# A gated MLP's down product, regrouped from plain block products into seven products of half blocks

## The chip, the cores and the metric

The kernel runs on one core of one Trainium2 chip. The metric is the device time of one execution in microseconds (us). Engines are named as in the profile: PE is TensorE (matmuls), PEld its weight load, DVE is VectorE, ACT is ScalarE, POOL is GpSimd, and SP is SyncE, which here only issues transfers.

## The reference, cut to what matters

The program is a decoder trunk of two layers over 1024 positions with a model width of 1024. Each layer mixes the sequence in four head groups, then runs a gated MLP with a short causal convolution, then adds a gated embedding. The part that is changed is the last matrix product of the MLP:

```python
D_MODEL, SEQ, DEPTH, D_FF = 1024, 1024, 2, 2816

def conv_ffn(x, w_up, conv_w, conv_b, w_down):
    up = x @ w_up                                  # 1024 -> 2 * 2816
    ...                                            # causal convolution over 3 positions
    gate, val = jnp.split(conv, 2, axis=-1)
    return (jax.nn.silu(gate) * val) @ w_down      # 2816 -> 1024

h = h + conv_ffn(rmsnorm(h, ffn_norm_g[i]), ...)
ple_gate = jax.nn.sigmoid(rmsnorm(h, ple_norm_g[i]) @ w_ple_gate[i])
h = h + ple_gate * (p[i] @ w_ple[i])
```

All inputs and the output are float32.

## The kernel before, in words

Everything is kept transposed: features lie on the 128 partitions, the 1024 positions along the free dimension, in two halves of 512. The 1024 model features are 8 blocks (index `m`), the 2816 hidden features are 22 blocks (`NFF`, index `f`).

Each float32 operand of a matmul is split in two parts that TensorE takes at its fast float32 rate: `hi`, a rounded copy, and `lo`, what the copy left over (`lo = x - hi`, helper `K.lo`, line 103, on whichever engine it is given). A product of two such operands is three matmuls: hi by hi, hi by lo, lo by hi (lines 1476 to 1478). One such matmul has a 128x128 block of weights and 512 positions.

`ffn_up` (lines 1304 to 1437) computes the up product. It already takes it as seven products of half blocks (`SEQ`, line 1301) instead of eight: sums of quarter blocks of weights and of activations are formed on VectorE, each of the seven is computed, and the results are recombined. It stores the 22 blocks of `hidden` in device memory (`hid`, line 1375).

`Down.load` (lines 1447 to 1463) prepares one of 44 operand sets: it issues the transfer of one 128x1024 block of `w_down` (tile `wr`, 512 KB) and of one 128x512 half block of `hid` (tile `g`, 256 KB), copies both hi parts on ScalarE, forms the `lo` of `g` on VectorE, and the `lo` of the weights in two halves on GpSimd. `Down.run` (lines 1465 to 1486) takes the left half of the positions and then the right one. For each it runs over the 22 blocks `f`, with 8 x 3 matmuls each into 8 PSUM banks; then VectorE adds the 8 banks to the residual tiles `h` (line 1484), and `done` hands each to the next normalization (`Norm.add`, lines 801 to 814: a scaled hi copy and a square on ScalarE, a `lo` part on VectorE, and sums of squares on VectorE and GpSimd in turn). After `Down.run` the gate product `pg` of the embedding follows (lines 762 to 764).

What sets the order of the work is the supply of tiles. Tiles come from pools with fixed numbers of buffers: 2 for `wr`, 6 for `wx` (the hi and lo of weights, two to a set, so 3 sets), 8 for the wide tiles that hold the pair hi and lo of `g` (also used by the convolution), 71 for half tiles (tag `h`), 8 PSUM banks. `T['dl']=4` is the number of sets that the code writes down ahead of the matmuls. The order on each engine is fixed when the program is built, from the order of the code and from what is then thought to be ready first; on the chip each engine runs its list in order and waits on semaphores.

Of the kernel before, what the change touches and what calls it, by code (L numbers as in the profile page):

```python
# [8 lines left out]
F32 = mybir.dt.float32  # L9
F32R = mybir.dt.float32r  # L10
# [4 lines left out]
ALU = mybir.AluOpType  # L15
# [4 lines left out]
P = 128  # L20
S = 1024
HS = 512
D = 1024
KD = D // P
DEPTH = 2
NFF = 22
# [15 lines left out]
T = dict(early=(0, 0.2), s5=((0.1, 0.7), (0.1, 0.7)), hgrn=((0.2, 0.92), (0.2, 0.92)), cd=((0.05, 0.85), (0.05, 0.85)), prep=((0.3, 1), (0.3, 1)), b=(0, 1), a=(0.9, 0.95), pre=(8, 10, 12, 13), vals=(5, 6), ahead=3, plv=4, mx=8, pw=1, rt=2, sc=2, rp=6, dl=4, qk=(4, 4), up=5)  # L42


class Kern:
    def __init__(self, tc, ctx, halves=71):
        self.tc, self.nc = tc, tc.nc
        self.n, self.turn = 0, False
        self.other = []
        self.cp = ctx.enter_context(tc.tile_pool(name="cp", bufs=1))  # L50
        self.sp = ctx.enter_context(tc.tile_pool(name="sp", bufs=2))
        self.pp = ctx.enter_context(tc.tile_pool(name="pp", bufs=2, space=PSUM))
        self.halves = halves
# [51 lines left out]
    def after(self, i, u):  # L105
        self.tc.add_manual_dep(i.ins, u.ins.name, mybir.DependencyInfo(
            mybir.DependencyClass.NoSync, mybir.DependencyReason.DATA), reason="order")
# [627 lines left out]
def rows(wh, wl, k, m=P):  # L735

    return wh[:, k * m:(k + 1) * m], wl[:, k * m:(k + 1) * m]

def wraw(K, src, n=S, blocks=1):
    raw = K.sp.tile([P, n], F32, name=K._nm("wr"), tag="wr", bufs=2)  # L740
    K.nc.sync.dma_start(raw if blocks == 1 else raw.rearrange("p (k m) -> p k m", k=blocks), src)
    return raw
# [36 lines left out]
class Norm:  # L779
# [11 lines left out]
    def add(self, i, n, x):  # L791
        self.parts(i, n, x)
        self.square(i, n, x)
# [77 lines left out]
def run(gen):  # L871
    for _ in gen:
        pass
# [149 lines left out]
def attention(heads):  # L1023
# [10 lines left out]
    for _ in b.prep():  # L1034
        yield
    run(a.values())
    for i in range(len(heads)):
        nxt, pre = get(i + 2), iter(())
        mx, vals = (b.max(), b.values()) if b else (iter(()), iter(()))
        for step, _ in enumerate(a.out()):  # L1040
            for _ in range(2 if step % 2 or step < T['mx'] else 1):
                next(mx, None)
            if step == 6 and nxt:
                while nxt() is None:
                    yield
                nxt = nxt()
                pre = nxt.prep()
            if step in T['pre']:
                next(pre, None)
            if step in T['vals']:  # L1050
                next(vals, None)
            yield
        for g in (mx, vals, pre):
            run(g)
        a, b = b, nxt
# [168 lines left out]
class Quarters:  # L1224
# [22 lines left out]
    def flush(self, n=0):  # L1247

        for t in self.todo[:len(self.todo) - n]:
            if len(t) == 4:  # L1250
                self.K.nc.scalar.copy(t[3], t[2])
            self.K.lo(*t[:4])
        self.todo = self.todo[len(self.todo) - n:]
        for t in self.todo:
            if len(t) == 4:
                self.K.nc.scalar.copy(t[3], t[2])
                t.append(True)
# [182 lines left out]
class Down:  # L1440

    def __init__(self, K, hid, w_down):
        self.K, self.hid, self.w, self.ops = K, hid, w_down, []

    def load(self):

        K, nc = self.K, self.K.nc
        V, G = nc.vector, nc.gpsimd  # L1450
        n, f = divmod(len(self.ops), NFF)
        if n == 2:
            return
        r, g = wraw(K, self.w[f]), K.h(name="g")
        nc.sync.dma_start(g, self.hid[f][:, n * HS:(n + 1) * HS])
        hi, lo = K.wx(), K.wx()
        gh, gl = K.pair(F32R, "g")
        nc.scalar.copy(gh, g)  # L1458
        nc.scalar.copy(hi, r)  # L1459
        K.lo(V, gl, g, gh)  # L1460
        for c in (slice(0, HS), slice(HS, S)):
            K.lo(G, lo[:, c], r[:, c], hi[:, c])
        self.ops.append(((hi, lo), (gh, gl)))

    def run(self, h, hdr, done):
        K, nc = self.K, self.K.nc
        V = nc.vector
        for n in range(2):
            ps = [b("dn") for b in (K.pf, K.pf, K.po, K.po, K.px, K.px, K.px, K.px)]
            for f in range(NFF):  # L1470
                while len(self.ops) < min(n * NFF + f + T['dl'], 2 * NFF):
                    self.load()
                w, (gh, gl) = self.ops[n * NFF + f]
                for m in range(KD):
                    ah, al = rows(*w, m)
                    nc.tensor.matmul(ps[m], lhsT=ah, rhs=gh, start=f == 0, stop=False)  # L1476
                    nc.tensor.matmul(ps[m], lhsT=ah, rhs=gl, start=False, stop=False)  # L1477
                    nc.tensor.matmul(ps[m], lhsT=al, rhs=gh, start=False, stop=f == NFF - 1)  # L1478
                m = f - NFF + KD + 4
                if 0 <= m < KD:  # L1480
                    h[m][n] = K.h(name="h")
                    nc.sync.dma_start(h[m][n], hdr[m][:, n * HS:(n + 1) * HS])
            for m in range(KD):
                V.tensor_tensor(h[m][n], h[m][n], ps[m], op=ALU.add)
            for m in range(KD):
                done(m, n)


@with_exitstack
def body(ctx, tc, xT, pT, pos, invf, sgn, vecs, prms, dsk, bfs, w_fm, w_misc, w_tm, w_uq, w_ukv, w_glu,  # L1490
# [29 lines left out]
    def first(l):  # L1520

        uf, z = [K.two(name="uf") for _ in range(2)], K.two(name="z")
        scaled = lambda t: lambda n, ps: V.tensor_tensor(t[n], ps, nm.r(n), op=ALU.mult)
        run(proj(K, [w_fm[l, i] for i in FIRST], nm.xs, [scaled(t) for t in uf + [z]], banks=[K.pf, K.pf, K.po],
                 ws=None if l else ws))
        return uf, z
# [413 lines left out]
```

## Time and profile before

| | |
|---|---|
| median of 3 runs | 3009.31 us (3005.92 to 3016.06) |
| the profiled execution's own time | 3008.91 us |
| its span in the trace | 3007.2 us |
| PE, PEld busy | 2819.5 us (94%), 2270.8 us (76%) |
| DVE, ACT, POOL busy | 2139.2 us (71%), 1417.9 us (47%), 1060.5 us (35%) |
| matmuls of `Down` (lines 1476 to 1478) | 3 x 704 |
| share of the chain that ended last | PE 61%, DVE 21% |

Busy time is the sum of an engine's instructions. Matmuls are pipelined, so one that is 390 ns long can start 227 ns after the one before it; the distance of starts is what counts for time. The chain is the work that ended last, followed back from the last instruction to what released it.

### The profile page before, as it was taken

The numbers are of one execution on the slowest core, as the hardware profiler recorded it, in microseconds if no ns is written. First come the engines' busy times: TensorE is split into PE (matmuls) and PEld (weight loads), VectorE is DVE, ScalarE is ACT, GpSimd is POOL, SyncE is SP. The second block draws the span as 40 slices with busy tenths as digits, with TensorE's granted clock in tenths as the row PEclk, the third lists the DMA queues.
The fourth block names the chain that finished last, engine by engine and source line by source line (L and its number), as shares of the span: only waits on it lengthen the run. The fifth ranks groups of instructions, "written<-read, shape, count | busy, mean of one in ns | idle before, by whom it ended". The sixth has DMA issues, their size and how long they took to land.

```text
span 3007.2 us, 37310 instructions
## 1 busy us (share of the span) xinstructions
PE 2819.5 (94%) x13346; PEld 2270.8 (76%) x13346; DVE 2139.2 (71%) x3130; ACT 1417.9 (47%) x2435; POOL 1060.5 (35%) x919
## 2 busy tenths in 40 slices
PE   8889899898999999999999898988989999999997
PEld 6777676676788888888787786766667888888886
DVE  7795767658999997253847776666599999953358
ACT  4235356665544444242733263666554444443345
POOL 2620123445322224555423201324452222255554
PEclk9898899999999999999998798999999999999998
DMA  3101011104222226353421011110132222262523
GB/s 127 38 23 43 29 59 56 38 8 148 70 84 85 84 85 207 98 192 98 156 67 32 21 50 49 57 55 22 46 126 74 85 84 85 77 221 94 190 102 130
DMA packets 115850, 255.14 MB, mean 85 GB/s; under 512 B 18544, under 2 KB 21232, under 8 KB 115664
## 3 DMA queue, kind: packets, MB, share of 16 engines
q1 hardware_dynamic: 114224, 252.10, 25.2%
q8 instruction: 105, 1.72, 0.2%
q10 hardware_dynamic: 1440, 0.65, 0.1%
q14 instruction: 81, 0.66, 0.1%
HBM read 197.58 MB, written 48.50 MB: 82 GB/s over the span
## 4 chain that ended last, share of the span: by engine, by line
PE 61%; DVE 21%; issue 8%; ACT 6%; POOL 3%; DMA 1%; SPq 0%; DVEq 0%; POOLq 0%; ACTq 0%
PE up L1358 8%; PE up L1356 8%; PE up L1357 8%; PE dn L1477 5%; PE dn L1476 5%; PE dn L1478 5%; PE qk L1006 2%; PE pj L774 2%; PE pj L775 2%; PE pj L776 2%; DVE wx L103 1%; DVE xq L1237 1%; PE ys L633 1%; DVE qz L286 1%; DVE bl L103 1%
## 5 line engine op out<-in xcount | busy, mean ns | idle before, releaser
L103 POOL TENSOR_TENSOR wx<-wr,wx 128x512 fp32r<-128x512 f32 (+1 forms) x293 | 485.9, 1671 | 351.0 <-ACT wx L1459 200.0
L1356 PE MATMUL up<-bh,wx 128*128 128x512 f32 x1232 | 481.3, 391 | 12.2 <-ACT wx L1349 12.2
L1357 PE MATMUL up<-bl,wx 128*128 128x512 f32 x1232 | 481.9, 391 | 8.6 <-POOL bl L103 4.5
L1358 PE MATMUL up<-bh,wx 128*128 128x512 f32 x1232 | 482.0, 391 | 6.3 <-DVE wx L103 6.3
L1356 PEld LDWEIGHTS up<-bh,wx 128*128 128x128 f32 x1232 | 232.6, 189 | 61.2 <-ACT wx L1349 13.1
L1477 PE MATMUL dn<-g,wx 128*128 128x512 f32 x704 | 274.7, 390 | 3.8 <-DVE g L103 3.8
L1357 PEld LDWEIGHTS up<-bl,wx 128*128 128x128 f32 x1232 | 232.7, 189 | 58.9 <-POOL bl L103 5.4
L103 POOL TENSOR_TENSOR pl<-pr,ph 128x512 fp32r<-128x512 f32 x144 | 164.3, 1150 | 314.9 <-ACT pr L1012 251.5
L1358 PEld LDWEIGHTS up<-bh,wx 128*128 128x128 f32 x1232 | 232.4, 189 | 56.5 <-DVE wx L103 8.3
L1476 PE MATMUL dn<-g,wx 128*128 128x512 f32 x704 | 274.6, 390 | 0.0
L1478 PE MATMUL dn<-g,wx 128*128 128x512 f32 x704 | 274.5, 390 | 0.0
L103 DVE TENSOR_TENSOR g<-g,g 128x512 fp32r<-128x512 f32 x88 | 105.1, 1210 | 204.5 <-ACT g L1458 196.2
L103 POOL TENSOR_TENSOR wx<-wq,wx 128x512 fp32r<-128x512 f32 x44 | 65.2, 1483 | 515.9 <-ACT wx L1349 515.9
L774 PE MATMUL pj<-xs,wx 128*128 128x512 f32 (+1 forms) x512 | 211.7, 414 | 15.3 <-ACT xs L801 7.0
L1459 ACT CAST wx<-wr 128x1024 fp32r<-128x1024 f32 x88 | 92.4, 1050 | 277.2 <-PE dn L1477 260.5
L775 PE MATMUL pj<-xs,wx 128*128 128x512 f32 (+1 forms) x512 | 207.2, 405 | 0.9 <-DVE xs L802 0.9
L776 PE MATMUL pj<-xs,wx 128*128 128x512 f32 (+1 forms) x512 | 207.0, 405 | 0.8 <-DVE wx L103 0.5
L1477 PEld LDWEIGHTS dn<-g,wx 128*128 128x128 f32 x704 | 132.6, 188 | 32.1 <-DVE g L103 4.7
L1476 PEld LDWEIGHTS dn<-g,wx 128*128 128x128 f32 x704 | 132.5, 188 | 27.8
L1478 PEld LDWEIGHTS dn<-g,wx 128*128 128x128 f32 x704 | 132.5, 188 | 27.5
L1367 DVE SCALAR_TENSOR_TENSOR cv<-u,vec,cv 128x1023 f32<-128x1023 f32 x88 | 131.0, 1491 | 28.1 <-ACT cv L1366 27.8
L103 POOL TENSOR_TENSOR yl<-xn,yh 128x512 fp32r<-128x512 f32 x24 | 35.8, 1493 | 293.8 <-ACT yh L862 293.8
(464 smaller groups left out, 6972.0 us busy)
## 6 DMA issues: line engine op xcount, KB each, us to landing
wr<-in_w_down SPq DMA_DIRECT2D x88, 512.0 KB
wr<-in_w_up SPq DMA_DIRECT2D x88, 256.0 KB
wq<-in_w_up SPq DMA_DIRECT2D x88, 256.0 KB
hid<-cv SPq DMA_DIRECT2D x44, 512.0 KB
g<-hid SPq DMA_DIRECT2D x88, 256.0 KB
wr<-in_w_fm SPq DMA_DIRECT2D x30, 512.0 KB
wr<-in_w_pg SPq DMA_DIRECT2D x28, 512.0 KB
hdr<-h SPq DMA_DIRECT2D x48, 256.0 KB
```

Of the source, the lines that this page charges most:

```text
L103: eng.tensor_tensor(out, x, hi.bitcast(F32), op=ALU.subtract)
L774: nc.tensor.matmul(out, lhsT=ah, rhs=bh, start=(i == 0), stop=False)
L775: nc.tensor.matmul(out, lhsT=ah, rhs=bl, start=False, stop=False)
L776: nc.tensor.matmul(out, lhsT=al, rhs=bh, start=False, stop=(i == n - 1))
L1356: nc.tensor.matmul(ps, lhsT=ah, rhs=bh, start=k == 0, stop=False)
L1357: nc.tensor.matmul(ps, lhsT=ah, rhs=bl, start=False, stop=False)
L1358: nc.tensor.matmul(ps, lhsT=al, rhs=bh, start=False, stop=k == KD // 2 - 1)
L1367: V.scalar_tensor_tensor(c[:, 1:], u[:, :S - 1], cw[:, 1:2], c[:, 1:], op0=ALU.mult, op1=ALU.add)
L1459: nc.scalar.copy(hi, r)
L1476: nc.tensor.matmul(ps[m], lhsT=ah, rhs=gh, start=f == 0, stop=False)
L1477: nc.tensor.matmul(ps[m], lhsT=ah, rhs=gl, start=False, stop=False)
L1478: nc.tensor.matmul(ps[m], lhsT=al, rhs=gh, start=False, stop=f == NFF - 1)
```

## The change

`Down` is rewritten as seven products too. The 22 blocks of hidden features are taken as 11 pairs `f` and `e = f + 11`, the 8 blocks of model features as two halves of 4, and the positions as two halves of 512. A set now belongs to one of four kinds, of 11 sets each: "12", "67" and "45" carry two products of half blocks each (24 matmuls to a set), "3" carries one (12 matmuls). All hi parts are made on ScalarE, all sums and all `lo` parts on VectorE; GpSimd has no part in it. The `lo` parts of a set are written down one load later than its hi parts (`todo`, `flush`). In kind "45" the sum of the two halves of the weights (`r[:, L] + r[:, R]`) stands in the load itself. The recombination of the results is spread over the steps as a list `later`, of which three entries are taken after each step.

The new code, cut to its core:

```diff
+    KINDS = ("12", "67", "45", "3")
     def load(self):
-        r, g = wraw(K, self.w[f]), K.h(name="g")
-        nc.sync.dma_start(g, self.hid[f][:, n * HS:(n + 1) * HS])
-        nc.scalar.copy(gh, g)
-        nc.scalar.copy(hi, r)
-        K.lo(V, gl, g, gh)
-        for c in (slice(0, HS), slice(HS, S)):
-            K.lo(G, lo[:, c], r[:, c], hi[:, c])
+        def both(c):
+            r = K.sp.tile([P, S], F32, name=K._nm("wr"), tag="wr", bufs=2)
+            ld(r[:, L], self.w[f][:, c])
+            ld(r[:, R], self.w[e][:, c])
+            return r
+        def hidden(i, n):
+            t = self.b[i, n] = K.h(name="g")
+            ld(t, self.hid[i][:, n * HS:(n + 1) * HS])
+            return t
+        todo, self.todo = self.todo, []
+        def part(o, ol, x):
+            nc.scalar.copy(o, x)
+            self.todo.append((V, ol, x, o))
+        if kind == "12":
+            r, q = both(L), K.two(name="q")
+            ld(q[0], self.w[f][:, R])
+            ld(q[1], self.w[e][:, R])
+            part(hi, lo, r)
+            s3, s2 = K.h(name="s3"), K.h(name="s2")
+            xs = hidden(f, 0), hidden(e, 0)
+            V.tensor_tensor(s3, r[:, L], q[0], op=ALU.subtract)
+            V.tensor_tensor(s2, q[1], s3, op=ALU.subtract)
+            self.s.append((s2, s3))
+        elif kind == "67":
+            s2, s3 = self.s[f]
+            b12, b22, t2 = hidden(f, 1), hidden(e, 1), self.b[f, 0]
+            V.tensor_tensor(b12, b22, b12, op=ALU.subtract)
+            part(hi[:, L], lo[:, L], s2)
+            part(hi[:, R], lo[:, R], s3)
+            V.tensor_tensor(t2, b12, t2, op=ALU.add)
+            xs = t2, b12
+        elif kind == "45":
+            r = both(R)
+            t1, t4, b22 = self.b[f, 0], self.b[e, 0], self.b[e, 1]
+            V.tensor_tensor(t4, t4, t1, op=ALU.subtract)
+            V.tensor_tensor(t1, b22, t1, op=ALU.subtract)
+            V.tensor_tensor(r[:, L], r[:, L], r[:, R], op=ALU.add)
+            part(hi, lo, r)
+            xs = t1, t4
+        else:
+            a12, s2 = K.h(name="a12"), self.s[f][0]
+            ld(a12, self.w[e][:, L])
+            V.tensor_tensor(s2, a12, s2, op=ALU.subtract)
+            part(hi[:, L], lo[:, L], s2)
+            xs = (self.b[e, 1],)
+        for x in xs:
+            gh, gl = K.pair(F32R, "g")
+            part(gh, gl, x)
+            bs.append((gh, gl))
+        flush()                      # the lo parts of the load before
     def run(self, h, hdr, done):
...
+                for j, (gh, gl) in enumerate(bs):
+                    for m in range(M):       # M = 4
+                        (ah, al), o = rows(*w, M * j + m), ps[M * j + m]
+                        nc.tensor.matmul(o, lhsT=ah, rhs=gh, start=f == 0, stop=False)
+                        nc.tensor.matmul(o, lhsT=ah, rhs=gl, start=False, stop=False)
+                        nc.tensor.matmul(o, lhsT=al, rhs=gh, start=False, stop=f == H - 1)
+                if kind == "12" and f >= H - M:
+                    hload(f - H + M, 0)
+                for _ in range(3):
+                    if later:
+                        later.pop(0)()
+            for m in range(M):
+                if kind == "12":
+                    p1[m] = K.h(name="p1")
+                    nc.scalar.copy(p1[m], ps[m])
+                elif kind == "67":
+                    V.tensor_tensor(p1[m], ps[m], p1[m], op=ALU.add)
+                elif kind == "45":
+                    p5 = K.h(name="p5")
+                    nc.scalar.copy(p5, ps[m])
+                    u3[m] = p5
+                else:
+                    add(m, 1, ps[m])
...
+                if kind == "12":
+                    add(m, 0, q)
+                    after(lambda m=m: add(m, 0, p1[m]))
+                elif kind == "67":
+                    u3[m] = K.h(name="u3")
+                    V.tensor_tensor(u3[m], q, p1[m], op=ALU.add)
+                else:
+                    add(M + m, 0, q)
+                    after(lambda m=m: done(M + m, 0), lambda m=m, x=u3[m]: add(M + m, 1, x),
+                          lambda m=m: done(M + m, 1), lambda m=m, x=u3[m]: add(m, 1, x))
+            if kind == "12":
+                after(*[lambda m=m: hload(M + m, 0) for m in range(M)])
+            elif kind == "67":
+                after(*[lambda m=m: hload(m, 1) for m in range(M)], *[lambda m=m: hload(M + m, 1) for m in range(M)])
+                for m in range(M):
+                    after(lambda m=m, x=u3[m]: add(M + m, 0, x), lambda m=m: add(m, 1, p1[m]),
+                          lambda m=m, x=u3[m]: add(M + m, 1, x), lambda m=m: done(m, 0))
```

Here `add(m, n, x)` is one VectorE addition of `x` to `h[m][n]`, and `hload` is the transfer of one residual tile.

## Rows read from the trace of the kernel before

**Rows 1.** Timeline of PE: start us, busy us, engine, line, operation, out<-in.

```profile
1169.70 0.39 PE L1476 MATMUL dn<-g,wx 128*128 128x512 f32 x1
...
1411.29 0.39 PE L762 MATMUL pg<-xs,wx 128*128 128x512 f32 x1
...
2650.04 0.39 PE L1476 MATMUL dn<-g,wx 128*128 128x512 f32 x1
...
2893.19 0.39 PE L762 MATMUL pg<-xs,wx 128*128 128x512 f32 x1
```

**Rows 2.** Timeline of ACT in Down; in brackets idle before, and its releaser.

```profile
1197.00 1.05 ACT L1459 CAST wx<-wr 128x1024 fp32r<-128x1024 f32 x1 [3.87 <-PE dn L1477]
1197.96 0.61 ACT L1458 CAST g<-g 128x512 fp32r<-128x512 f32 x1
1202.44 1.05 ACT L1459 CAST wx<-wr 128x1024 fp32r<-128x1024 f32 x1 [3.87 <-PE dn L1477]
```

**Rows 3.** Groups by line, 1169.5 to 1411.3 us: busy, mean ns | idle, releasers.

```profile
L1477 PE MATMUL dn<-g,wx 128*128 128x512 f32 x352 | 137.1, 389 | 1.9 <-DVE g L103 1.9
...
L103 POOL TENSOR_TENSOR wx<-wr,wx 128x512 fp32r<-128x512 f32 (+1 forms) x86 | 129.3, 1524 | 107.7 <-ACT wx L1459 99.0 <-PE dn L1478 5.7 <-PE up L1358 3.0
...
L103 DVE TENSOR_TENSOR g<-g,g 128x512 fp32r<-128x512 f32 x42 | 50.2, 1212 | 99.0 <-ACT g L1458 90.9 <-DMA wr<-in_w_down 8.1
```

**Rows 4.** Busy by stretch: length, PE, PEld, DVE, ACT, POOL, PEclk, DMA share, GB/s.

```profile
1169.50:1411.30 241.80, 239.87 (x1059) 198.29 (x1058) 88.66 (x78) 80.01 (x107) 134.33 (x89) 1.00 0.47 154
...
1055.00:1075.00 20.00, 20.00 (x90) 16.56 (x89) 19.29 (x22) 7.58 (x11) 4.09 (x3) 1.00 0.30 106
```

**Rows 5.** Timeline of DVE at the end of ffn_up and within Down.

```profile
1134.70 1.22 DVE L1374 TENSOR_TENSOR cv<-cv,cv 128x1024 f32<-128x1024 f32 x1
1135.83 2.31 DVE L1367 SCALAR_TENSOR_TENSOR cv<-u,vec,cv 128x1023 f32<-128x1023 f32 x1
...
1146.19 0.68 DVE L103 TENSOR_TENSOR wx<-s,wx 128x512 fp32r<-128x512 f32 x1
1146.79 0.68 DVE L1381 TENSOR_TENSOR u<-up,s 128x512 f32<-128x512 f32 x1
...
1214.92 1.37 DVE L103 TENSOR_TENSOR g<-g,g 128x512 fp32r<-128x512 f32 x1 [4.07 <-ACT g L1458]
```

**Rows 6.** Timeline of POOL at the end of ffn_up.

```profile
1155.88 2.05 POOL L103 TENSOR_TENSOR wx<-wq,wx 128x512 fp32r<-128x512 f32 x1 [13.70 <-ACT wx L1349]
```

**Rows 7.** Groups by line, 1169.5 to 1411.3 us: the norm after Down.

```profile
L802 DVE SCALAR_TENSOR_TENSOR xs<-h,vec,xs 128x512 fp32r<-128x512 f32 x9 | 13.3, 1498 | 0.0
...
L814 POOL TENSOR_TENSOR sq<-sq,sq 128x512 f32<-128x512 f32 x3 | 5.1, 1704 | 0.1
```

**Rows 8.** Busy by stretch, at the start of Down and later in it.

```profile
1180.00:1200.00 20.00, 20.00 (x90) 16.57 (x89) 10.96 (x11) 7.95 (x11) 11.79 (x9) 1.00 0.95 311
...
1220.00:1240.00 20.00, 20.00 (x90) 16.55 (x89) 5.47 (x4) 5.04 (x7) 11.84 (x8) 1.00 0.25 86
```

**Rows 9.** Timeline of SP, which issues the transfers, at the start of Down.

```profile
1162.14 0.33 SPq L741 DMA_DIRECT2D wr<-in_w_down  x1
1162.52 2.33 SPq L1455 DMA_DIRECT2D g<-hid  x5
...
1174.10 0.33 SPq L741 DMA_DIRECT2D wr<-in_w_down  x1
```

**Rows 10.** Timeline of ACT: the casts of the blocks sent for in Rows 9.

```profile
1167.17 1.06 ACT L1459 CAST wx<-wr 128x1024 fp32r<-128x1024 f32 x1 [4.38 <-PE up L1358]
...
1182.62 1.04 ACT L1459 CAST wx<-wr 128x1024 fp32r<-128x1024 f32 x1
```

**Rows 11.** Timeline of PE where the second layer's right half begins.

```profile
2788.33 0.50 PE L1477 MATMUL dn<-g,wx 128*128 128x512 f32 x1 [1.90 <-DVE g L103]
```

**Rows 12.** Busy by stretch around Rows 11.

```profile
2786.00:2788.00 2.00, 0.43 (x2) 0.00 (x1) 2.00 (x3) 1.94 (x4) 0.52 (x1) 1.00 0.33 66
2788.00:2790.00 2.00, 1.67 (x5) 1.33 (x6) 2.00 (x3) 0.68 (x1) 1.25 (x2) 0.69 0.91 323
2790.00:2792.00 2.00, 2.00 (x7) 1.51 (x6) 2.00 (x2) 0.80 (x2) 1.72 (x2) 0.50 1.01 302
```

More of the change, by code (lines that the diff above doesn't have):

```diff
@@ L1440 @@
 class Down:
+    KINDS = ("12", "67", "45", "3")
     def __init__(self, K, hid, w_down):
         self.K, self.hid, self.w, self.ops = K, hid, w_down, []
+        self.b, self.s, self.todo = {}, [], []
     def load(self):
         K, nc = self.K, self.K.nc
-        V, G = nc.vector, nc.gpsimd
-        n, f = divmod(len(self.ops), NFF)
-        if n == 2:
+        V, H = nc.vector, NFF // 2
+        kind, f = divmod(len(self.ops), H)
+        if kind == len(self.KINDS):
             return
-        r, g = wraw(K, self.w[f]), K.h(name="g")
@@ L1455, in load @@
-        nc.sync.dma_start(g, self.hid[f][:, n * HS:(n + 1) * HS])
+        kind, e = self.KINDS[kind], f + H
+        L, R = slice(0, HS), slice(HS, S)
+        ld = nc.sync.dma_start
         hi, lo = K.wx(), K.wx()
-        gh, gl = K.pair(F32R, "g")
-        nc.scalar.copy(gh, g)
-        nc.scalar.copy(hi, r)
-        K.lo(V, gl, g, gh)
-        for c in (slice(0, HS), slice(HS, S)):
-            K.lo(G, lo[:, c], r[:, c], hi[:, c])
-        self.ops.append(((hi, lo), (gh, gl)))
+        def both(c):
[3 more added lines that the diff above has]
+            return r
@@ new lines, in hidden, with flush @@
+        def hidden(i, n):
[6 more added lines that the diff above has]
+            self.todo.append((V, ol, x, o))
+        def flush():
+            for t in todo:
+                K.lo(*t)
+        if kind == "12":
[30 more added lines that the diff above has]
+            xs = (self.b[e, 1],)
@@ L1465, in run @@
+        bs = []
+        for x in xs:
[3 more added lines that the diff above has]
+        flush()
+        self.ops.append(((hi, lo), bs))
+        if len(self.ops) == len(self.KINDS) * H:
+            todo = self.todo
+            flush()
     def run(self, h, hdr, done):
@@ L1467, in run @@
         V = nc.vector
[L1468 to L1471, printed above, removed]
-                    self.load()
[L1473 to L1486, printed above, removed]
+        H, M = NFF // 2, KD // 2
@@ new lines, in run, with hload, add, after @@
+        HV = (slice(0, HS), slice(HS, S))
+        later, p1, u3 = [], [None] * M, [None] * M
+        def hload(m, n):
+            h[m][n] = K.h(name="h")
+            nc.sync.dma_start(h[m][n], hdr[m][:, HV[n]])
+        def add(m, n, x):
+            V.tensor_tensor(h[m][n], h[m][n], x, op=ALU.add)
+        def after(*fs):
+            later.extend(fs)
+        for i, kind in enumerate(self.KINDS):
+            ps = [b("dn") for b in (K.pf, K.pf, K.po, K.po, K.px, K.px, K.px, K.px)[:KD if kind != "3" else M]]
+            for f in range(H):
+                at = i * H + f
+                while len(self.ops) < min(at + T['dl'], len(self.KINDS) * H):
+                    self.load()
+                w, bs = self.ops[at]
+                for j, (gh, gl) in enumerate(bs):
[21 more added lines that the diff above has]
+                    add(m, 1, ps[m])
+            if kind == "3":
+                for m in range(M):
+                    done(m, 1)
+                continue
+            for m in range(M):
+                q = ps[M + m]
+                if kind == "12":
[12 more added lines that the diff above has]
+                after(*[lambda m=m: hload(m, 1) for m in range(M)], *[lambda m=m: hload(M + m, 1) for m in range(M)])
+                for m in range(M):
+                    after(lambda m=m, x=u3[m]: add(M + m, 0, x), lambda m=m: add(m, 1, p1[m]),
+                          lambda m=m, x=u3[m]: add(M + m, 1, x), lambda m=m: done(m, 0))
```

## The prediction

> **What bounds the kernel now.** I read the timeline of PE first, to frame the stage that is rewritten, then the groups by line within that frame, then the busy time by stretch, and last the timelines of the feeding engines. The stage runs from the first `dn` matmul to the first `pg` matmul: 1411.29 - 1169.70 = 241.59 us in the first layer and 2893.19 - 2650.04 = 243.15 us in the second, 484.7 us together [rows 1]. Within it PE waits for nothing but one 1.9 us stall, where the right half begins [rows 3]. ScalarE's casts come exactly 5.44 us apart and are released by PE [rows 2]: one set of 24 matmuls takes 5.44 us, so matmuls start 0.2267 us apart, and 1056 of them are 239.4 us. VectorE is busy 88.7 us of the 241.8 and ScalarE 80.0 [rows 4]. So the stage is bound by the number of matmuls; the feeders have slack, GpSimd included (129.3 us of lo parts) [rows 3].
>
> **The change part by part.**
>
> *Matmuls.* Removed: 44 x 24 = 1056 for a layer. Added: 11 x (24 + 24 + 24 + 12) = 924. At 0.2267 us that is 209.5 us. If the new stage has no stall, it saves 241.59 - 209.5 = 32.1 us in the first layer and 33.7 us in the second, 65.8 us in all.
>
> *VectorE.* This is where the bill goes. In units of one 512-column tensor_tensor, a load costs 6 in "12" (two differences, a 1024-column lo as two, two lo of the hidden parts), 6 in "67", 7 in "45" and 3 in "3": 11 x 22 = 242 units. The recombination in `run` adds 8 + 8 + 12 + 4 + 8 + 4 = 44. A unit is 0.60 us where VectorE runs without a break (1146.19 to 1146.79; the 1024-column op takes 1.13 until the next starts) and 1.37 us beside GpSimd [rows 5]. GpSimd was idle in that first stretch, 13.70 us up to 1155.88 [rows 6], and the new stage gives it nothing but sums of squares, so I take 0.60: 286 x 0.60 = 172 us. The 16 `done` calls stay; their lo parts average 1.50 us in a crowd [rows 7], at most 24 us. Together 172 to 196 us, against 209.5 us of PE: 82 to 94%. At the other end, all units at 1.37 us would be 392 us.
>
> The Trainium skill, "SBUF — State Buffer", section "🔬 SBUF: two separate sides", says that VectorE with two SBUF inputs and GpSimd lock each other out of a shared port pair for a whole instruction. Rows 5 agree (0.68 against 1.37 us for the same operation). By that rule the low price holds wherever GpSimd is silent, and the sum stays as it is; a blend of both prices at the old mean of 1.21 us [rows 3] would give 346 us and a slower kernel.
>
> That VectorE can run nearly full beside a full PE is seen in `ffn_up`, which is built the same way: 19.29 us of 20 busy with PE at 20.00 [rows 4]. It is not even over the stage. "12" and "67" need 3.6 us of each 5.44; "45" needs 46.2 us for loads, about 14.4 for additions and 6 for `done`, some 67 in 59.8 us; "3" some 32 in 29.9. The sums of "45" and "3" read tiles that are already on the core, so they can go early, into the 20 us that "67" leaves free.
>
> *ScalarE.* By rows 2 a set needs 1.05 + 2 x 0.61 = 2.27 us of 5.44 (four casts of 0.61 in "67"; half that in "3"): about 90 us, plus eight copies out of PSUM and the old `done` work. It has room; I cost it at nothing. *GpSimd* loses 88 lo parts a layer, none of which PE waited for: nothing.
>
> *Transfers.* Before, 768 KB a set. Now "12" fetches six pieces of 256 KB, 1.57 MB, which at 5.44 us a set is 289 GB/s; the other kinds need a third of that or less. The queue has moved 311 GB/s at a busy share of 0.95 [rows 8], so the first eleven sets fit, with 7% to spare, and the transfers start before the matmuls do. Later stages relax to what rows 8 show as 86 GB/s and a bit more. SP issues 137 transfers instead of 104 a layer, at 0.33 to 0.47 us each [rows 9], some 60 us of its 210. A price is in the latency: a weight block was asked for at 1162.14 and cast at 1167.17, another at 1174.10 and cast at 1182.62 [rows 9, 10], so 5.0 to 8.5 us under such load. Three sets of `wx` let weights be made two sets, 10.9 us, ahead of PE.
>
> *New seams.* Before, PE had one seam (left half to right half) where all 8 banks are emptied, VectorE is full and the next operands come late. Now there are four: the entry (three heavy loads instead of one light one, while the last convolutions are still on VectorE), "12" to "67", "67" to "45", and "3", whose sets are only 2.72 us long. What one costs is in the trace: 1.9 us [rows 3], and in the second layer the same 1.90 us [rows 11] with the granted clock at 0.69 and 0.50 just after [rows 12], by which that layer is 243.15 - 241.59 = 1.56 us longer, 3.46 us in all. Bounds: none stalls (0 us), or each costs 3.46 us (13.8 us a layer). I take 1.9 us for each, since most banks have over 4 us between their last matmul and their next use: 7.6 us a layer, 15.2 us.
>
> The Trainium skill, "TensorE: Matmul & The Clock Gate", section "What's actually happening", says that the clock follows how busy PE has been. Rows 12 agree: after the idle stretch it fell from 2.4 to 1.2 GHz. A stall that keeps coming back would then be paid twice, which is one more reason not to put the range's top at the seams alone.
>
> *Sum*, against the profiled execution: 3008.9 - 65.8 + 15.2 = 2958.3 us. That execution stands 0.4 us below the median of the runs shown, so no correction is due. Forecast: 2958 us, with its own range from 2943 (no seam stalls) to 2971 (all at 3.46 us).
>
> **The rivals.**
>
> *A: VectorE becomes the bound in "45" and "3".* For it: the 67 + 32 = 99 us counted above against 89.7 us of PE, and an engine that runs in order with waits (at the 96% of rows 4, 103 us). Add the GpSimd sums of squares, 1.7 us each [rows 7], six a layer, each holding up a VectorE op by about 0.77 us (1.37 - 0.60), 4.6 us. Excess 103 + 4.6 - 89.7 = 18 us a layer, on top of 4 us for the other seams: 22 us, 44 in all, 2943 + 44 = 2987 us. Against it: VectorE's free time in "67", if the fixed order uses it. Chance 0.20.
>
> *B: the ring of the two weight buffers paces "12", and the kernel gets slower or stays.* The code writes the differences of the next load ahead of this load's lo part. If VectorE's list keeps that order, a `wr` buffer is freed only after the next load has landed, and transfers and VectorE follow each other in a ring: latency plus two differences (1.2 us) plus a lo part (1.13 us), for every set. With 8.5 us of latency that is 10.8 us a set: 11 x 10.8 - 59.8 - 10.9 us of lead = 48 us a layer, so 2943 + 96 = 3039 us. With 5.0 us it is 7.3 us a set, 9.9 us a layer, 2963 us. It eats the whole gain from 9.4 us a set ((32.9 + 59.8 + 10.9) / 11), which is 7.1 us of latency. For it: "12" asks for 289 GB/s, near what the queue can do. Against it: this load's lo part is ready as soon as its cast is done, usually before the next load lands, so an order built by readiness puts it first. Chance 0.12 that it costs 25 us a layer or more.
>
> **How the numbers follow.** Forecast 0.64, A 0.20, B 0.12, and 0.04 for less than 2943 us, if the gate product after the stage also gains from VectorE's earlier norm work. A measurement of this kernel can tell about 0.3%, 9 us, from no change: below 3000 is faster, above 3018 slower. The forecast, A and the small case are all faster, nearly 0.86 with A's upper tail just over; B gives 0.05 for no change and 0.09 for slower. The range that holds 8 in 10 goes from the floor less 3 us to where A ends: 2940 to 3002 us.
>
> **What would show it.** In the new trace: 924 `dn` matmuls a layer, and 217 us from the first of them to the first `pg` matmul. VectorE's lo parts near 0.68 us on average, not 1.2, and no lo part of `Down` on GpSimd. In the first 60 us of the stage some 290 GB/s with PE full. Short PE waits at the seams, released by VectorE. A is right if PE waits for VectorE again and again in the last 90 us; B if it waits all along in "12", with VectorE in turn waiting for transfers and the clock at its lower level. The forecast is wrong if the stage takes 225 us or more in either layer, or under 209.

## The result and the profile after

The changed kernel takes 2962.57 us in the median (2957.34 to 2966.82, 4 runs) against 3007.61 us (3005.67 to 3016.06) for the kernel before: a ratio of 0.9844, with a 95% interval from 0.9816 to 0.9872. That is 1.6% faster. The profiled execution took 2966.12 us, 42.8 us less than the profiled one of before.

First the page of the changed kernel: span, then busy time of each engine, its share of the span and its instructions.

```profile
span 2964.4 us, 37115 instructions
...
PE 2771.1 (93%) x13082; PEld 2227.8 (75%) x13082; DVE 2341.3 (79%) x3538; ACT 1460.2 (49%) x2539; POOL 813.7 (27%) x743
```

PE lost 48 us of work, GpSimd 247 us, and VectorE took on 202 us. The frame of the stage, answering to [rows 1], is again the timeline of PE:

```profile
1169.61 0.39 PE L1556 MATMUL dn<-g,wx 128*128 128x512 f32 x1
...
1393.46 0.39 PE L762 MATMUL pg<-xs,wx 128*128 128x512 f32 x1
...
2629.65 0.39 PE L1556 MATMUL dn<-g,wx 128*128 128x512 f32 x1
...
2852.23 0.39 PE L762 MATMUL pg<-xs,wx 128*128 128x512 f32 x1
```

The stage takes 1393.46 - 1169.61 = 223.85 us in the first layer and 222.58 us in the second, 446.4 us together against 484.7 us: 38.3 of the 42.8 us. Another 2.6 us are between the first layer's `pg` and the second layer's `dn`, and 1.9 us behind the second layer's `pg`.

The groups by line of the changed kernel, 1169.5 to 1393.5 us, answer to [rows 3]: busy, mean ns | idle before, releasers.

```profile
L1557 PE MATMUL dn<-g,wx 128*128 128x512 f32 x308 | 121.6, 395 | 3.3 <-DVE g L103 3.3
L1558 PE MATMUL dn<-g,wx 128*128 128x512 f32 x308 | 120.9, 397 | 5.6 <-DVE wx L103 5.5
...
L103 DVE TENSOR_TENSOR g<-g,g 128x512 fp32r<-128x512 f32 x73 | 49.0, 686 | 11.2 <-ACT g L1478 11.2
...
L103 DVE TENSOR_TENSOR wx<-wr,wx 128x1024 fp32r<-128x1024 f32 x21 | 25.6, 1218 | 2.4 <-ACT g L1478 2.4
...
L1492 DVE TENSOR_TENSOR s<-wr,q 128x512 f32<-128x512 f32 x8 | 5.5, 693 | 7.4 <-DMA wr<-in_w_down 7.4
```

Three things are to be seen. There are 3 x 308 = 924 matmuls. A lo part costs VectorE 686 ns where it cost 1212 ns [rows 3]. And PE now waits 8.9 us for lo parts, while VectorE itself waits 7.4 us for weight transfers at line 1492, the first difference of kind "12". The busy time by stretch (length, PE, PEld, DVE, ACT, POOL, PEclk, DMA share, GB/s), answering to [rows 4, 8, 12]:

```profile
1169.60:1393.50 223.90, 215.00 (x926) 174.51 (x925) 191.47 (x280) 103.31 (x162) 17.95 (x6) 0.98 0.45 152
...
1180.00:1190.00 10.00, 6.67 (x21) 5.03 (x21) 9.79 (x12) 3.99 (x7) 0.00 (x0) 0.72 0.53 186
1190.00:1200.00 10.00, 10.00 (x42) 8.20 (x42) 6.83 (x10) 2.99 (x4) 0.00 (x0) 0.94 0.90 294
1230.00:1290.00 60.00, 60.00 (x266) 49.70 (x265) 59.82 (x99) 29.41 (x51) 0.00 (x0) 1.00 0.27 98
1330.00:1340.00 10.00, 7.64 (x33) 6.01 (x33) 6.50 (x9) 2.19 (x3) 0.00 (x0) 1.00 0.28 84
1370.00:1380.00 10.00, 9.17 (x40) 7.19 (x40) 10.00 (x16) 5.90 (x10) 2.30 (x2) 1.00 0.00 1
```

PE has holes in three places: at the entry (1180 to 1190), inside kind "45" (1330 to 1340), and in kind "3" (1370 to 1380). It has none in kind "67" (1230 to 1290), where VectorE is busy for 59.82 of 60 us. The length of each kind, from its first matmul to the first of the next, says how much each lost (us, first layer / second layer; 264 matmuls, or 132 in "3", times 0.2267 us is the length without a stall):

| | "12" | "67" | "45" | "3" | stage |
|---|---|---|---|---|---|
| without a stall | 59.84 | 59.84 | 59.84 | 29.92 | 209.44 |
| changed kernel | 66.02 / 64.06 | 59.84 / 59.84 | 64.17 / 64.85 | 33.82 / 33.83 | 223.85 / 222.58 |

So 14.4 and 13.1 us a layer are lost, 27.5 us together. The timeline of VectorE at the entry shows the place of the first loss (in brackets: idle before, and its releaser):

```profile
1170.70 1.22 DVE L103 TENSOR_TENSOR wx<-wr,wx 128x1024 fp32r<-128x1024 f32 x1
...
1175.66 0.69 DVE L1492 TENSOR_TENSOR s<-wr,q 128x512 f32<-128x512 f32 x1 [3.15 <-DMA wr<-in_w_down]
1176.27 1.28 DVE L1367 SCALAR_TENSOR_TENSOR cv<-u,vec,cv 128x1023 f32<-128x1023 f32 x1
...
1185.06 1.89 DVE L103 TENSOR_TENSOR g<-g,g 128x512 fp32r<-128x512 f32 x3
...
1187.76 1.22 DVE L103 TENSOR_TENSOR wx<-wr,wx 128x1024 fp32r<-128x1024 f32 x1
...
1191.86 0.69 DVE L1492 TENSOR_TENSOR s<-wr,q 128x512 f32<-128x512 f32 x1 [0.47 <-DMA wr<-in_w_down]
1192.47 1.22 DVE L103 TENSOR_TENSOR wx<-wr,wx 128x1024 fp32r<-128x1024 f32 x1
...
1198.44 0.69 DVE L1492 TENSOR_TENSOR s<-wr,q 128x512 f32<-128x512 f32 x1 [1.11 <-DMA wr<-in_w_down]
1199.05 1.22 DVE L103 TENSOR_TENSOR wx<-wr,wx 128x1024 fp32r<-128x1024 f32 x1
```

Beside it the timeline of SP, which issues the transfers of `wr`:

```profile
1171.98 0.33 SPq L1465 DMA_DIRECT2D wr<-in_w_down  x1
...
1189.04 0.33 SPq L1465 DMA_DIRECT2D wr<-in_w_down  x1
...
1193.71 0.33 SPq L1465 DMA_DIRECT2D wr<-in_w_down  x1
```

Read together they are a ring. A lo part ends at 1187.76 + 1.22 = 1188.98 and frees its `wr` buffer; the transfer of the next load but one is issued at 1189.04; VectorE's next instruction on weights is that load's difference, which has to wait until 1191.86; only behind it stands the lo part of the load before, at 1192.47; it frees the next buffer, and SP issues at 1193.71. One turn takes 4.71 us, the next 6.58 us, against 5.44 us that PE needs for a set. At 1175.66 the convolutions behind the waiting difference were held up too (3.15 us), and behind them the `lo` parts at 1185.06 that PE was waiting for. The stall of PE that came of it, in the timeline of PE:

```profile
1180.49 1.98 PE L1556 MATMUL dn<-g,wx 128*128 128x512 f32 x8
1185.79 0.79 PE L1557 MATMUL dn<-g,wx 128*128 128x512 f32 x1 [3.33 <-DVE g L103]
1186.38 0.63 PE L1558 MATMUL dn<-g,wx 128*128 128x512 f32 x1
1186.81 0.63 PE L1557 MATMUL dn<-g,wx 128*128 128x512 f32 x1
1187.23 0.63 PE L1558 MATMUL dn<-g,wx 128*128 128x512 f32 x1
```

After the 3.33 us the matmuls start 0.43 us apart where they otherwise start 0.2267 us apart, with a granted clock of 0.72 over these 10 us: half speed, 1.2 of 2.4 GHz, for a part of them.

In kind "45" the same ring stands at line 1509, the sum of the two weight halves. VectorE, then PE and SP of the changed kernel:

```profile
1330.27 1.22 DVE L103 TENSOR_TENSOR wx<-wr,wx 128x1024 fp32r<-128x1024 f32 x1
...
1336.01 0.69 DVE L1509 TENSOR_TENSOR wr<-wr 128x512 f32<-128x512 f32 x1 [1.14 <-DMA wr<-in_w_down]
1336.61 1.22 DVE L103 TENSOR_TENSOR wx<-wr,wx 128x1024 fp32r<-128x1024 f32 x1
```

```profile
1331.55 0.73 PE L1558 MATMUL dn<-g,wx 128*128 128x512 f32 x2 [1.52 <-DVE wx L103]
...
1337.89 0.73 PE L1558 MATMUL dn<-g,wx 128*128 128x512 f32 x2 [0.83 <-DVE wx L103]
```

```profile
1331.56 0.33 SPq L1465 DMA_DIRECT2D wr<-in_w_down  x1
...
1337.90 0.33 SPq L1465 DMA_DIRECT2D wr<-in_w_down  x1
```

From lo part to lo part it is 1336.61 - 1330.27 = 6.34 us: 4.45 us from issue to the sum (1331.56 to 1336.01), 0.60 for the sum, 1.22 for the lo part and 0.07 until SP issues. That is 0.90 us more than PE's 5.44 us, and PE waits 0.83 us in that set.

### The profile page after: what moved, and what is told of

It reads as the page before. It is cut to its first block, busy times and chain, and to the rows that moved or that the text cites. A ratio compares the mean times of both kernels' runs of the same rounds, so it can differ in the third digit from the quotient of the medians.

```text
span 2964.4 us, 37115 instructions
## 1 busy us (share of the span) xinstructions
PE 2771.1 (93%) x13082; PEld 2227.8 (75%) x13082; DVE 2341.3 (79%) x3538; ACT 1460.2 (49%) x2539; POOL 813.7 (27%) x743
## 5 line engine op out<-in xcount | busy, mean ns | idle before, releaser
L103 POOL TENSOR_TENSOR wx<-wr,wx 128x512 fp32r<-128x512 f32 (+1 forms) x117 | 225.1, 1925 | 119.2 <-ACT wx L1349 66.1
L1558 PE MATMUL dn<-g,wx 128*128 128x512 f32 x616 | 241.9, 397 | 10.9 <-DVE wx L103 10.8
L1557 PE MATMUL dn<-g,wx 128*128 128x512 f32 x616 | 243.1, 395 | 5.6 <-DVE g L103 5.6
L1556 PE MATMUL dn<-g,wx 128*128 128x512 f32 x616 | 238.2, 390 | 0.0
L814 POOL TENSOR_TENSOR sq<-sq,sq 128x512 f32<-128x512 f32 x52 | 91.7, 1763 | 524.2 <-ACT sq L808 522.6
L103 DVE TENSOR_TENSOR wx<-wr,wx 128x1024 fp32r<-128x1024 f32 (+2 forms) x153 | 161.3, 1055 | 46.5 <-ACT wx L750 37.0
L1558 PEld LDWEIGHTS dn<-g,wx 128*128 128x128 f32 x616 | 116.7, 191 | 41.9 <-DVE wx L103 17.7
L1478 ACT CAST g<-g 128x512 fp32r<-128x512 f32 x154 | 93.4, 620 | 99.6 <-PE dn L1558 56.5
L1557 PEld LDWEIGHTS dn<-g,wx 128*128 128x128 f32 x616 | 117.6, 191 | 31.1 <-DVE g L103 6.5
L1349 ACT CAST wx<-s 128x512 fp32r<-128x512 f32 x88 | 54.1, 622 | 172.1 <-DVE s L1336 98.9
```

The costliest lines, as they stand in the source:

```text
L103: eng.tensor_tensor(out, x, hi.bitcast(F32), op=ALU.subtract)
L1478: nc.scalar.copy(o, x)
L1556: nc.tensor.matmul(o, lhsT=ah, rhs=gh, start=f == 0, stop=False)
L1557: nc.tensor.matmul(o, lhsT=ah, rhs=gl, start=False, stop=False)
L1558: nc.tensor.matmul(o, lhsT=al, rhs=gh, start=False, stop=f == H - 1)
```

## The experiments

The theory was that the order of VectorE's list costs the 14 us: the next load's first sum, which waits for its transfer, stands ahead of this load's lo part, which is ready. Rivals: the transfers are too slow or too late in themselves; VectorE simply has too much work in these places; the seams cost what they cost because banks have to be emptied, as the prediction had it. Each line below gives median, ratio to the kernel before on the same chip with its 95% interval, and the kinds as in the table above (first layer / second layer).

The stage is what to read, for the rest of the program, unchanged in nearly all of these kernels, differs from run to run. The changed kernel was run once more for this, as it is:

> The change as made, once more on the same chip as the run beside it, as the yardstick for small differences: 2957 to 2967 us, the stage 223 us a layer, with "12" and "45" at 64 to 66 us and "3" at 33.8.

It took 2965.6 us, 0.9857 [0.9838, 0.9876]; stage 221.76 / 225.69, with "12" at 64.0 / 66.5, "45" at 64.1 / 65.5 and "3" at 33.8 in both layers: losses of the same size in the same places, though the larger loss at the entry now stands in the second layer. But from the first layer's `pg` to the second layer's `dn` it needed 1241.24 us where the first profile of the same kernel shows 1236.19, and its stage began 3.0 us later. So differences below some 8 us between whole times are not read.

**The lo parts of the load before, first.** The one place in `load` where they are written moves from its end to its start:

```diff
+        flush()
         if kind == "12":
...
-        flush()
         self.ops.append(((hi, lo), bs))
```

> The lo parts of the load before are written down ahead of this load's sums, so that VectorE's list has them first; the work itself is the same. Ring theory (VectorE runs in order and a lo part waits behind the first use of the next load's transfer; that makes the stalls at the entry, 6.3 and 3.7 us, and at the end of "45", 3.3 and 3.7 us): most of these 17 us go, 2946 to 2955 us, and VectorE no longer waits for transfers between a cast and its lo part. Capacity theory (VectorE simply has too much work): nothing changes, 2959 to 2966 us.

2939.89 us (2938.76 to 2950.15), 0.9783 [0.9769, 0.9797]: 22.7 us less than the changed kernel. Kinds: 60.92 / 60.59, 59.84 / 59.84, 59.84 / 59.83, 33.06 / 34.13; stage 213.66 / 214.39. Nothing was added or taken away, so it is the order that cost 18.4 us in the two stages together. What is left in "3" is one stall of 2.40 us in each layer; in the second layer matmuls 0.43 us apart follow it, in the first they do not, so "3" takes 34.13 us there against 33.06. The two stalls in the timeline of PE:

```profile
1368.27 0.50 PE L1558 MATMUL dn<-g,wx 128*128 128x512 f32 x1 [2.40 <-DVE wx L103]
...
2811.22 0.80 PE L1558 MATMUL dn<-g,wx 128*128 128x512 f32 x1 [2.40 <-DVE wx L103]
```

VectorE's timeline of this kernel shows the other order (its L1493 and L1510 are L1492 and L1509 of the changed kernel):

```profile
1187.91 1.22 DVE L103 TENSOR_TENSOR wx<-wr,wx 128x1024 fp32r<-128x1024 f32 x1
1189.04 0.69 DVE L1493 TENSOR_TENSOR s<-wr,q 128x512 f32<-128x512 f32 x1
...
1327.11 0.69 DVE L1510 TENSOR_TENSOR wr<-wr 128x512 f32<-128x512 f32 x1 [3.44 <-DMA wr<-in_w_down]
1327.72 1.22 DVE L103 TENSOR_TENSOR wx<-wr,wx 128x1024 fp32r<-128x1024 f32 x1
```

In "12" the lo part now stands ahead of the difference. In "45" VectorE still waits 3.44 us for a transfer, and PE loses nothing by it (59.84 us): a wait in the list matters only when something ready is shut in behind it.

**A third `wr` buffer.** The order stays; the ring gets one more place, paid for with two half tiles:

```diff
-    def __init__(self, tc, ctx, halves=71):
+    def __init__(self, tc, ctx, halves=69):
...
-            r = K.sp.tile([P, S], F32, name=K._nm("wr"), tag="wr", bufs=2)
+            r = K.sp.tile([P, S], F32, name=K._nm("wr"), tag="wr", bufs=3)
```

> Three raw weight buffers instead of two, paid for with two of the 71 half tiles. Ring theory: the next block can be sent for one load earlier, so VectorE finds it there; the 17 us of stalls at the entry and at the end of "45" shrink to a few, 2947 to 2956 us. Capacity theory: no change, 2959 to 2966 us. Cost of the two half tiles: up to 3 us.

2961.63 us, 0.9845 [0.9833, 0.9858], no gain in the whole: the time is the one that the capacity theory gave. But the stage is cured as well: 60.13 / 60.26, 59.84, 59.84, 33.85 / 33.85, together 213.66 / 213.79, and no difference of "12" waits for a transfer of `wr` any more (the waits that are left, 0.7 us at most, are for `q`). Of the 19.0 us that the stages gained, 11.2 us were lost elsewhere in the profiled run: the first stage began 4.3 us later, and the stretch from `pg` to the second stage took 6.9 us more, 1243.11 us; the rest shows as a span 7.8 us shorter. The buffers are shared with `ffn_up`, so the edit may cost there, but the changed kernel itself was seen at 1241.24 us: which of the two it is stays open. For the ring it is a clear answer: with two buffers and this order the lap is too long, with three it is not, and the transfers themselves are fast enough.

**The sum of "45" back to where it was one step later.** Sum, cast and lo part of the weights of "45" are done in the next load:

```diff
-            V.tensor_tensor(r[:, L], r[:, L], r[:, R], op=ALU.add)
-            part(hi, lo, r)
+            self.wsum.append((hi, lo, r))      # sum, cast and lo in the next load's flush
```

> Undoes the last part of the change: in kind "45" the sum of the weights, its cast and its lo part come one load later. Ring theory: the sum's wait for its transfer no longer stands ahead of the last lo part in VectorE's list, but the cast comes later too: within 5 us either way, with the end of "45" changed and the entry (6.3 and 3.7 us) as it is. Capacity theory: the same work, no change at all, 2959 to 2966 us.

2953.19 us (2951.16 to 2962.0), 0.9824 [0.981, 0.9837]. Kinds: 62.04 / 66.03, 59.84, 59.84 / 59.84, 33.81 / 33.81; stage 215.53 / 219.52. The loss of "45" is gone, that at the entry remains (2.2 / 6.2 us). The time is 9.4 us below the changed kernel's, more than either theory gave. So this one part of the change, the sums made a step sooner, costs 4.3 and 5.0 us a layer in the order in which it stands, and its removal is worth less in the whole time than can be told (the intervals meet). With the lo parts first it costs nothing.

**The weights' lo parts on GpSimd.** The hidden parts' lo stays on VectorE:

```diff
-        def part(o, ol, x):
+        def part(o, ol, x, eng=V):
             nc.scalar.copy(o, x)
-            self.todo.append((V, ol, x, o))
+            self.todo.append((eng, ol, x, o))
...
-            part(hi, lo, r)
+            part(hi, lo, r, G)                 # and so for s2, s3 of the other kinds
```

> The lo parts of the weights go back to GpSimd, 77 halves of 512 columns a layer, some 46 us of VectorE at 0.60. Capacity theory: VectorE is relieved, "3" loses its 2.5 to 3 us a layer of stalls: 2952 to 2960 us. Price theory of the prediction (VectorE's operation costs 1.37 us beside GpSimd): what is left on VectorE gets dearer, its lo and sum operations average over 0.9 us, and the stage gets longer: 2970 to 3000 us. Ring theory: a weight buffer is freed later, since GpSimd takes 1.5 us for 512 columns; more stalls in "12".

3019.47 us, 1.0044 [1.0029, 1.0059]: slower than before, and slower than any of the theories gave. Kinds: 73.59 / 74.85, 70.48 / 71.71, 67.56 / 66.42, 38.81 / 38.64; stage 250.44 / 251.62, though VectorE has over 50 operations fewer in it. The groups by line of this kernel, 1167.4 to 1417.8 us:

```profile
L1558 PE MATMUL dn<-g,wx 128*128 128x512 f32 x308 | 125.0, 406 | 13.6 <-POOL wx L103 13.6
...
L103 DVE TENSOR_TENSOR g<-g,g 128x512 fp32r<-128x512 f32 x73 | 68.5, 949 | 24.0 <-ACT g L1478 23.8
L103 POOL TENSOR_TENSOR wx<-s,wx 128x512 fp32r<-128x512 f32 x33 | 62.1, 1896 | 47.2 <-PE dn L1558 29.5 <-ACT wx L1478 7.2 <-PE dn L1557 7.0
```

The same lo part on VectorE costs 949 ns where GpSimd works beside it and 686 ns where it doesn't. One on GpSimd takes 1896 ns, and PE waits 13.6 us for GpSimd's lo parts. So two things lengthen the stage, GpSimd's own slow lo parts and VectorE's dearer operations, and this run doesn't part them. With the lo parts of the weights on GpSimd, the seven products take longer (250.44 us) than the eight did (241.59 us).

**The lo part right behind its cast, in its own load.**

```diff
         def part(o, ol, x):
             nc.scalar.copy(o, x)
-            self.todo.append((V, ol, x, o))
+            K.lo(V, ol, x, o)
```

> The other way to free the lo parts: each is written down right behind its own cast, with nothing kept for the next load. Ring theory: VectorE's list again has this load's lo part ahead of the next load's sums, so the stage is as short as with lo parts first, 212 to 216 us a layer, 2938 to 2950 us in all. If only the one order of writing that was tried before is good: 2955 us or more.

2946.76 us (2935.41 to 2956.03), 0.9799 [0.9774, 0.9825]. Kinds: 59.91 / 61.19, 59.84, 59.84, 33.10 / 33.13; stage 212.69 / 213.99. A second way of getting the lo part ahead of the next wait, with the same stage. The delay of the lo parts by one load, which the code does by hand, is not needed.

**Two entries of `later` a step in "3", with the lo parts first.**

```diff
-                for _ in range(3):
+                for _ in range(3 if kind != "3" else 2):
```

> Lo parts first, and in kind "3" only two entries of the recombination are taken after a step instead of three. Capacity theory for what is left (one 2.4 us stall a layer late in "3", where VectorE is full): the stall goes, the stage is 211 us, 2 to 5 us less than with lo parts first. Rival (that stall is an order of the list too, and the rest of the list only shifts): within 2 us of it.

2938.1 us (2934.46 to 2939.18), 0.9776 [0.9759, 0.9793]. Kinds: 60.82 / 60.56, 59.84, 59.84, 29.92 / 29.92; stage 210.42 / 210.16. The loss in "3" is gone to the last hundredth, and PE waits 0.6 us in the whole first stage. By stretch, the stage and its end in this kernel:

```profile
1169.55:1379.97 210.42, 209.78 (x926) 173.35 (x924) 189.28 (x278) 101.19 (x160) 10.38 (x5) 1.00 0.46 158
...
1349.55:1379.97 30.42, 30.42 (x136) 25.16 (x135) 30.42 (x45) 17.30 (x30) 8.28 (x4) 1.00 0.03 9
```

VectorE is busy for all of the last 30.42 us, which hold "3", and PE too. This kernel is the best of all here, by the stage. Part of the gain is paid back right behind it: the first gate product takes 89.91 us instead of 88.80, with a wait of PE of 0.82 us that the changed kernel doesn't have, and behind the second layer's `pg` it is 1.2 us more. Its whole time can't be told from that of the first experiment. The same edit without the lo parts first:

> The change as made, with only the taking of two entries a step instead of three in kind "3"; the lo parts stay where they are. If the stalls are three separate causes that add up: "3" falls from 33.8 to 29.9 us, "12" (64 to 66) and "45" (64 to 65) stay, the stage is 219 to 220 us a layer, 2951 to 2958 us. If the order of the lo parts lies behind "3" too: "3" stays at 33 us or more and nothing changes.

2964.49 us, 0.9859 [0.9833, 0.9884]; "3" still takes 32.07 / 32.02 us, with "12" at 62.68 / 66.1 and "45" at 64.51 / 65.15. Neither forecast came out: "3" falls, but not to 29.9 us. So neither edit alone clears "3" (33.06 / 34.13 with the order alone), and the two together do. Why the pacing alone leaves 2.1 us is not shown. That VectorE comes to "3" late after the stalls of "45" would be one reason; but with the third buffer, and with the sum of "45" a step later, "45" has no stall, and "3" takes 33.8 us as in the changed kernel.

**How long the feeders need by themselves.** The lo parts first, and of each three matmuls one is left out (hi by lo where `m` is even, lo by hi where it is odd), 616 a layer:

```diff
-                        nc.tensor.matmul(o, lhsT=ah, rhs=gl, start=False, stop=False)
-                        nc.tensor.matmul(o, lhsT=al, rhs=gh, start=False, stop=f == H - 1)
+                        if m % 2:
+                            nc.tensor.matmul(o, lhsT=ah, rhs=gl, start=False, stop=f == H - 1)
+                        else:
+                            nc.tensor.matmul(o, lhsT=al, rhs=gh, start=False, stop=f == H - 1)
```

> Lo parts first, with two of the three matmuls of each product (the lo terms are taken in turn, so the result lacks half of them): PE needs 139.7 us a layer, and what feeds it shows its own length. If VectorE's busy time (190 us) is the next bound: 190 to 200 us a layer. If the transfers of "12" or the weight buffers are: longer in "12", where VectorE then waits for transfers; if both have room: 145 to 160 us.

One run: 2899.22 us; stage 191.47 / 192.48. The 616 matmuls alone would be 139.6 us. By stretch in this kernel:

```profile
1165.25:1356.72 191.47, 161.58 (x617) 122.81 (x616) 186.07 (x278) 99.55 (x160) 23.68 (x6) 0.90 0.50 174
...
1165.25:1225.25 60.00, 53.98 (x210) 41.43 (x209) 56.75 (x80) 32.53 (x49) 0.00 (x0) 0.91 0.97 348
```

Now VectorE is the bound, with 186.07 of 191.47 us busy; in the first 60 us the transfers are nearly full beside it, with a share of 0.97. The stage is 18 us below the 209.44 us of PE: the room that VectorE has, 9%.

**The weights' hi parts on VectorE as well**, with the lo parts first:

```diff
-        def part(o, ol, x):
-            nc.scalar.copy(o, x)
+        def part(o, ol, x, w=False):
+            V.tensor_copy(o, x) if w else nc.scalar.copy(o, x)      # w for weights
```

> Lo parts first, with the hi parts of the weights cast by VectorE instead of ScalarE: 22 casts of 1024 columns at about 0.69 us and 33 of 512 at about 0.4 us, 28 us more on VectorE a layer, 218 us with the 190 it has. Capacity theory: VectorE becomes the bound, the stage takes 220 to 228 us a layer, 2952 to 2972 us. If only the order of the list counts: 214 us a layer, as before, 2938 to 2948 us.

2961.11 us (2952.93 to 2965.59), 0.9855 [0.983, 0.9881]: against the first experiment 21 us lost. Kinds: 60.29 / 62.38, 59.84, 59.84, 35.57 / 35.82; stage 215.54 / 217.88. The stage and the added casts:

```profile
1177.23:1392.77 215.54, 211.74 (x926) 172.86 (x924) 212.69 (x331) 64.05 (x107) 23.63 (x5) 1.00 0.45 155
...
L1479 DVE CAST wx<-wr 128x1024 fp32r<-128x1024 f32 x20 | 13.7, 684 | 0.8 <-PE dn L1560 0.8
...
L1479 DVE CAST wx<-s 128x512 fp32r<-128x512 f32 x33 | 12.8, 416 | 0.3 <-PE dn L1560 0.3
```

With 26.5 us more of casts VectorE is busy for 212.69 of 215.54 us, and the backlog comes out in "3". Of the 21 us the stages explain 5.4 us; the profiled run's first stage began 8.9 us later and the stretch between the stages took 2.8 us more. So ScalarE for the hi parts is right, and by the stages it is worth some 3 us a layer.

## Why the prediction was right

The time, 2962.57 us, lies 5 us above the forecast of 2958, well within its own range of 2943 to 2971. The trade of matmuls for VectorE work was right; one term of the sum was mis-sized and put in the wrong places, and that the time came so close is in part luck. The stages lost 27.5 us against 15.2 us forecast: 18.4 us by the order of VectorE's list, 7.5 us by the pacing of "3" (446.4 to 428.0 to 420.6 us in the experiments) and 1.7 us that are left. By one of its own signs it stood at the edge: it would be wrong with a stage of 225 us or more, and the changed kernel's stages take 223.85 and 222.58 us in one run, 221.76 and 225.69 us in the other.

*Matmuls: right.* 924 of them at 0.2267 us. Kind "67" takes 59.84 us in both layers, which is 264 x 0.2267 us exactly, and with order and pacing mended the whole stage comes to 210.4 and 210.2 us.

*VectorE: right.* 172 to 196 us were forecast, 191.47 us are in the trace, and 186.07 us where nothing holds it up. The price of 0.60 us for a start to the next (0.68 us of record) rested on GpSimd's silence; the run with GpSimd at work gave 949 instead of 686 ns. The Trainium skill, "SBUF — State Buffer", section "🔬 SBUF: two separate sides", describes an exclusive lock between the two engines for a whole instruction; the two means agree with it. As an estimate, it is as if over a third of the operations had met the other engine at the full price of 1.37 us ((949 - 686) / (1370 - 686) = 0.38).

*Early sums: right for the hidden parts of "45" alone.* VectorE is busy for 59.82 of 60 us within "67", and 20 of the 22 sums of hidden parts for "45" stand there (first layer). But the weight sums of "45" and the sums of "3" do not read tiles that are already on the core, as the prediction had it: each reads a weight block that is fetched for it. Of the former 2 of 11 stand in "67", of the latter none.

*Transfers: right.* The first 60 us moved 283 GB/s, against 289 forecast, with PE busy for 56.67 us of them.

*New seams: the step that failed.* The prediction took 1.9 us for each of four seams, where banks are emptied, 7.6 us a layer. The seams "12" to "67" and "67" to "45" cost nothing: "67" begins, runs and ends without a stall. The entry cost 6.2 / 4.2 us, the middle of "45", which is no seam, 4.3 / 5.0 us, and "3" 3.9 / 3.9 us: 14.4 and 13.1 us. The stages together came to 446.4 us against 2 x 209.5 + 15.2 = 434.2 us, 12.2 us over. The clock's part of it is in the trace of the entry: the stall of 3.33 us is followed by matmuls 0.43 us apart, and the granted clock falls to 0.72. The Trainium skill, "TensorE: Matmul & The Clock Gate", section "What's actually happening", ties the clock to how busy PE has been of late; this stretch agrees. The first layer's stalls in "45", of 1.52 and 0.83 us, left the granted clock at 1.00 (1330 to 1340).

*Rival B: the mechanism was real, the argument against it wrong.* The prediction said that an order built by readiness puts the lo part first. VectorE's list has the next load's difference first, all through "12" and "45". What kept the rival small is the latency: 2.8 us (1189.04 to 1191.86) to 4.7 us (1193.71 to 1198.44) from issue to use, where 5.0 to 8.5 us was reckoned with. Those two figures were not latencies: of the casts in [rows 10] one was released by PE and the other follows its engine's work without a wait, so they only bound the latency from above, and the blocks were of 512 KB, while a difference here waits for a piece of 256 KB. So a turn took 4.7 to 6.6 us, close to PE's 5.44, instead of 7.3 to 10.8, and the loss was some 9 us a layer, which is where the prediction's low price for the rival lay (9.9 us), and not 48. Three different edits (order, lo part in its own load, third buffer) each take the stage to between 212.7 and 214.4 us: that the ring causes the losses in "12" and "45" is shown.

*Rival A: true of "3" alone.* The sign that the prediction gave for it, PE waiting for VectorE again and again in the last 90 us, did come; but so it does in a ring, and the sign can't tell the two apart. "45" does not need more of VectorE than there is, for with the lo parts first it runs without a stall; "3" does, as it was paced, and two entries a step instead of three clear it, once the lo parts stand first.

*The small case: a gain behind the stage, but not by the way it gave.* The time did not fall below 2943 us. The first gate product (first `pg` to first `pj`) took 90.9 us before and 88.8 us after, where the prediction named VectorE's earlier norm work as a reason. In the trace of before, PE waits in it for GpSimd, twice:

```profile
1446.74 0.50 PE L764 MATMUL pg<-xs,wx 128*128 128x512 f32 x1 [0.43 <-POOL wx L103]
...
1486.17 0.50 PE L764 MATMUL pg<-xs,wx 128*128 128x512 f32 x1 [1.06 <-POOL wx L103]
```

In the changed kernel PE waits for nothing there. Why GpSimd is now in time is not shown: with the lo parts of the weights back on it, this product took 88.8 us as well. With the 2.6 and 1.9 us found outside the stages, that took back 4.4 of the 12.2 us (before rounding): 2958.3 + 12.2 - 4.4 = 2966.1 us, which is the profiled execution.

What stays open is why the unchanged parts of the program differ between runs, by 3.0 us ahead of the first stage and 5.0 us behind it for one and the same kernel; no experiment was made for it.

## What to carry to other kernels

On an engine that runs its list in order, ask of every instruction that waits for a transfer what stands behind it and whose buffer that work would free: an order by hand or by a planner that puts the next load's first use ahead of this load's last use turns two buffers into one, and the period becomes latency plus work. The price of a VectorE operation depends on what GpSimd does beside it (686 ns against 949 ns here), so a plan that moves work to VectorE should count on a quiet GpSimd in the same stretch, or on the higher price. Where the count of matmuls gives the length of each kind of step without a stall, set the measured lengths beside it one by one: the loss is then seen where it is, and not where a seam was expected.

## What the runs showed of the hardware

- Transfers came faster than [rows 8] let one expect: 348 GB/s over 60 us at a DMA share of 0.97, when PE had less to do and the feeders set the pace, against 311 GB/s there. The 7% that the prediction left between 289 and 311 GB/s was no limit.
- At the start of the stage, with 294 GB/s moved (1190 to 1200), a 256 KB piece of a weight block was in use 2.8 to 4.7 us after its issue.
- Two stalls of PE of the same length, 2.40 us, in the same place of the two layers (lo parts first, kind "3"): around the one the granted clock is 1.00 (1366 to 1372), around the other 0.72 (2809 to 2815).
- VectorE and PE can both be without a gap for 30 us (30.42 of 30.42 each) and nearly so for 60 us (59.82 and 60.00), with ScalarE at half load beside them.
- The same kernel's unchanged stretch of some 1240 us took 1236.2 us in one run and 1241.2 us in another, and over all kernels that leave it alone 1229.6 to 1241.2 us.
